# Rotary embedding on one core: first slab loaded in two pieces, the tables behind its first piece on the sync queue, last slab stored in two pieces

## The chip, the cores and the metric

The kernel runs on one core of one Trainium2 chip. The metric is the device time of one execution in microseconds, lower is better; a kernel's time is the median of its runs. Beside the times there is a profile of one execution, taken by the hardware profiler: when each engine's instructions ran, what released them from a wait, and what the DMA engines moved. Times inside a profile count from the start of its span, the first instruction on the core.

## The reference

The input `x` has the shape (8, 2048, 8, 64) in float32: batch, sequence, heads, head dimension. `cos` and `sin` are (2048, 32). Each head's vector of 64 is split into two halves, which are rotated by the position's angles:

```
x1 = x[..., : 32]
x2 = x[..., 32 :]
cos = cos[None, :, None, :]
sin = sin[None, :, None, :]
out1 = x1 * cos - x2 * sin
out2 = x1 * sin + x2 * cos
return concatenate([out1, out2], axis=-1)
```

Input and output are 33.55 MB each, the two tables 0.26 MB each (256 KB). Every element is read once and written once, with three arithmetic operations on it.

## The kernel before

**Tiling.** The sequence of 2048 is cut into 128 partitions of 16 rows each (`R`). One row of a partition is one position: 8 heads of 64, `HD` = 512 floats. Half of a partition's rows (`SL` = 8) of one batch is a slab: 128 partitions by `SLAB` = 4096 floats, 2 MB. There are 16 slabs, numbered 0 to 15 and called x0 to x15 below; their stores are called s0 to s15. Half a slab, `UNIT` = 2048 floats per partition, is 1 MB; `2 * HD` is 512 KB and `HD` is 256 KB.

**Loads.** `load(i)` takes one of `NBUF` = 9 buffers (`xt`) and issues the loads of slab i on the sync queue (SP, line 84), cut as `cuts(i)` says (lines 62 to 65): x0 in 256, 256, 512 and 1024 KB, each other slab in one load of 2 MB. Behind the first piece of x0 the sync queue issues the sin table (line 89). The cos table is issued on the scalar engine's queue (ACT, line 92), ahead of everything else there. Lines 93 and 94 load the first nine slabs at once; slab 9 and those after it are loaded by line 200, when the store of the slab that had the buffer has landed.

**Preparation.** POOL builds an identity matrix (lines 96 and 97). ACT makes `nsin` = -sin (line 106), `neye` (line 107) and `sin_ps`, a copy of sin in PSUM (line 109); DVE copies cos to PSUM as `cos_ps` (line 108).

**Rotation.** `rotate(i, lo, n)` works on one piece of a slab, in place. `pieces(i)` (lines 67 to 72) gives the pieces: x0 in 256, 256, 512 and 1024 KB, x15 in 1024, 512, 256 and 256 KB, every other slab in two of 1 MB. A piece of the usual kind "A" takes four instructions. Two are on POOL (line 138): the halves of `t2`, x times sin and x times -sin with the halves exchanged. Two are on DVE: `t1` = x times cos (line 144) and then `xt` = `t1` + `t2` (line 151). The sum needs both POOL results. `t2` has three buffers, `t1` one in PSUM.

Slabs 5 and 10 are done in another way (`kinds`, lines 114 to 116): their first half is of kind "C" (DVE makes both products, lines 144 and 161), the second of kind "B" (POOL makes `t2` as before), and in both the sum is made on the tensor engine by multiplying with the identity (lines 156, 157, 172, 173), chunk by chunk of 512 floats, and ACT copies each chunk back into `xt` (lines 158 and 176).

**Stores.** `store` issues on the ACT queue (line 183), behind what ACT has been given before it. The loop at line 189 issues the store of slab i - 2 (`LAG` = 2) after the rotation of slab i. So s8 stands on ACT behind the 16 copies of slab 10, and s3 behind the 16 copies of slab 5. In the last round (slab 15) s13 and s14 are issued first, and then each piece of x15 right after its rotation. `keep` holds DVE's and ACT's instructions in program order.

Of the kernel before, what the change touches and what calls it, by code (L numbers as in the profile page):

```python
# [10 lines left out]
def kernel(  # L11
# [7 lines left out]
    nc = tc.nc  # L19
# [7 lines left out]
    HD = H * D  # L27
# [4 lines left out]
    SLAB = SL * HD  # L32
    UNIT = 4 * HD
# [5 lines left out]
    cos_src = cos.rearrange("(q r) d -> q r d", q=P)  # L39
# [10 lines left out]
    cos_sb = const_pool.tile([P, R, Dh], f32, tag="cb")  # L50
# [8 lines left out]
    last = len(slabs) - 1  # L59
    xts = {}  # L60

    def cuts(i):
        if i == 0:
            return [HD, HD, 2 * HD, UNIT]
        return [SLAB]

    def pieces(i):
        if i == 0:
            return [HD, HD, 2 * HD, UNIT]
        if i == last:  # L70
            return [UNIT, 2 * HD, HD, HD]
        return [UNIT, UNIT]

    def spans(sizes):
        lo = 0
        for n in sizes:
            yield lo, n
            lo += n

    def load(i):  # L80
        b, l = slabs[i]
        xt = xpool.tile([P, SLAB], f32, tag="xt", name=f"xt{i}")
        for lo, n in spans(cuts(i)):
            nc.sync.dma_start(
                out=xt[:, lo : lo + n],
                in_=xv[b, :, l * SLAB + lo : l * SLAB + lo + n],
            )
            if i == 0 and lo == 0:
                nc.sync.dma_start(out=sin_sb, in_=sin_src)
        xts[i] = xt  # L90

    nc.scalar.dma_start(out=cos_sb, in_=cos_src)
    for i in range(NBUF):
        load(i)

# [2 lines left out]
        out=eye,  # L98
        in_=eye,
# [80 lines left out]
    def store(i, lo, n):  # L180
        b, l = slabs[i]
        keep(
            nc.scalar.dma_start(  # L183
                out=ov[b, :, l * SLAB + lo : l * SLAB + lo + n],
                in_=xts[i][:, lo : lo + n],
            )
        )

    for i in range(last + 1):
        if i == last:  # L190
            for k in range(i - LAG, i):
                store(k, 0, SLAB)
        for lo, n in spans(pieces(i)):
            rotate(i, lo, n)
            if i == last:
                store(i, lo, n)
        if LAG <= i < last:
            store(i - LAG, 0, SLAB)
        if i > LAG and i - LAG - 1 + NBUF <= last:
            load(i - LAG - 1 + NBUF)  # L200
# [30 lines left out]
```

## Time and profile before

| | |
|---|---|
| median of 4 runs | 164.67 us (164.51 to 164.78) |
| the profiled execution's own time | 164.64 us |
| its span, first to last instruction | 162.9 us |
| DVE busy | 143.4 us, 88% of the span |
| POOL busy | 139.4 us, 86% |
| PE busy | 33.0 us, 20% |
| ACT busy | 12.0 us, 7% |
| moved by DMA | 67.66 MB, mean 415 GB/s over the span |
| loads | 15 of 2 MB, one of 1 MB, one of 512 KB, two of 256 KB; cos and sin 256 KB each |
| stores | 15 of 2 MB, one of 1 MB, one of 512 KB, two of 256 KB |
| DVE, 128x2048: product L144 / sum L151 | 2.293 / 2.292 us |
| DVE, 128x1024: product / sum | 1.229 / 1.225 us |
| DVE, 128x512: product / sum | 0.696 / 0.692 us |
| POOL L138, for a piece of 1 MB / 512 KB / 256 KB | 2.34 / 1.26 / 0.72 us each of two |

Engines are named as in the profile: PE is the tensor engine, DVE the vector engine, ACT the scalar engine, POOL the GpSimd engine, SP the sync engine; a name with q at its end is that engine's sequencer, where DMAs are issued. The row of tenths divides the span into 40 equal slices; a 9 in the row DMA means that the core's 16 DMA engines were busy for 90% of the slice or more. A line of a timeline gives start and duration in us, the engine, the line of the kernel, output and inputs, and in brackets how long the engine had been idle before it and what released it. A DMA's time "to landing" runs from its issue until its completion is signalled.

### The profile page before, as it was taken

The numbers are of one execution on the slowest core, as the hardware profiler recorded it, in microseconds if no ns is written. First come the engines' busy times: TensorE is split into PE (matmuls) and PEld (weight loads), VectorE is DVE, ScalarE is ACT, GpSimd is POOL, SyncE is SP. The second block draws the span as 40 slices with busy tenths as digits, with TensorE's granted clock in tenths as the row PEclk, the third lists the DMA queues.
The fourth block names the chain that finished last, engine by engine and source line by source line (L and its number), as shares of the span: only waits on it lengthen the run. The fifth ranks groups of instructions, "written<-read, shape, count | busy, mean of one in ns | idle before, by whom it ended". The sixth has DMA issues, their size and how long they took to land. (4 is left out here: it accounts for less than half of the span.)

```text
span 162.9 us, 480 instructions
## 1 busy us (share of the span) xinstructions
PE 33.0 (20%) x64; PEld 13.3 (8%) x64; DVE 143.4 (88%) x71; ACT 12.0 (7%) x20; POOL 139.4 (86%) x74
## 2 busy tenths in 40 slices
PE   0000000000000079991000000799940000000000
PEld 0000000000000024440000000234410000000000
DVE  0587999999999999999899999999999999999900
ACT  3300000000000002421000000023220000000000
POOL 1699999999999999799999999956999999995000
PEclk9999999999999999999655555569995555555555
DMA  5999999999999999999999999999999999999995
GB/s 143 390 437 435 427 378 431 435 427 431 439 427 431 431 435 431 427 431 435 427 433 427 433 431 435 427 435 427 435 431 431 427 431 439 427 431 439 419 411 214
DMA packets 5763, 67.66 MB, mean 415 GB/s; under 512 B 640, under 2 KB 640, under 8 KB 1664
## 3 DMA queue, kind: packets, MB, share of 16 engines
q1 hardware_dynamic: 2880, 33.82, 49.6%
q10 hardware_dynamic: 2880, 33.82, 48.8%
q14 instruction: 3, 0.02, 0.0%
HBM read 34.08 MB, written 33.55 MB: 415 GB/s over the span
## 5 line engine op out<-in xcount | busy, mean ns | idle before, releaser
L138 POOL TENSOR_TENSOR t<-xt,sin_sb 128x1024 f32<-128x1024 f32 (+2 forms) x34 | 70.9, 2086 | 10.8 <-DVE xt L151 6.3
L144 DVE TENSOR_TENSOR t<-xt,cos_ps 128x2048 f32<-128x2048 f32 (+2 forms) x36 | 73.9, 2056 | 1.0
L138 POOL TENSOR_TENSOR t<-xt,nsin 128x1024 f32<-128x1024 f32 (+2 forms) x34 | 71.0, 2088 | 0.0
L151 DVE TENSOR_TENSOR xt<-t,t 128x2048 f32<-128x2048 f32 (+2 forms) x32 | 64.8, 2025 | 5.6 <-POOL t L138 2.1
L172 PE MATMUL o<-t,eye 128*128 128x512 f32 x16 | 11.1, 784 | 86.7 <-DVE t L144 86.7
L176 ACT COPY xt<-o 128x512 f32<-128x512 f32 x8 | 4.7, 586 | 95.2 <-PE o L173 95.2
L172 PEld LDWEIGHTS o<-t,eye 128*128 128x128 f32 x16 | 3.7, 244 | 91.4 <-issue 91.4
L156 PE MATMUL o<-t,eye 128*128 128x512 f32 x16 | 8.2, 592 | 0.0
L157 PE MATMUL o<-t,eye 128*128 128x512 f32 x16 | 8.2, 592 | 0.0
L173 PE MATMUL o<-t,neye 128*128 128x512 f32 x8 | 6.2, 862 | 0.2 <-DVE t L161 0.2
L158 ACT COPY xt<-o 128x512 f32<-128x512 f32 x8 | 4.7, 586 | 9.0 <-PE o L157 9.0
L108 DVE COPY cos_ps<-cos_sb 128x512 f32<-128x512 f32 x1 | 0.7, 694 | 4.9 <-DMA cos_sb<-in_cos_dram 4.9
L161 DVE TENSOR_TENSOR t<-xt,sin_ps 128x2048 f32<-128x2048 f32 x2 | 4.6, 2280 | 0.0
L173 PE MATMUL o<-t,eye 128*128 128x512 f32 x8 | 4.1, 592 | 0.0
L157 PEld LDWEIGHTS o<-t,eye 128*128 128x128 f32 x16 | 3.0, 190 | 3.8 <-issue 3.8
L156 PEld LDWEIGHTS o<-t,eye 128*128 128x128 f32 x16 | 3.0, 190 | 3.8 <-issue 3.8
L173 PEld LDWEIGHTS o<-t,neye 128*128 128x128 f32 x8 | 2.1, 287 | 4.8 <-issue 3.2
L173 PEld LDWEIGHTS o<-t,eye 128*128 128x128 f32 x8 | 1.5, 190 | 1.9 <-issue 1.9
L106 ACT ACT_TABLE_LOAD x1 | 1.3, 1283 | 1.2 <-PEq L215 1.2
L106 ACT ACTIVATE nsin<-sin_sb 128x512 f32<-128x512 f32 x1 | 0.6, 630 | 3.1 <-DMA sin_sb<-in_sin_dram 3.1
L109 ACT COPY sin_ps<-sin_sb 128x512 f32<-128x512 f32 x1 | 0.6, 579 | 0.0
L96 POOL MEMSET eye<- 128x128 f32 x1 | 0.2, 205 | 0.3 <-POOLq L215 0.3
(6 smaller groups left out, 1.0 us busy)
## 6 DMA issues: line engine op xcount, KB each, us to landing
xt<-in_x_dram SPq DMA_DIRECT2D x15, 2048.0 KB, 28.3
out_dram<-xt ACTq DMA_DIRECT2D x15, 2048.0 KB, 15.1
xt<-in_x_dram SPq DMA_DIRECT2D x1, 1024.0 KB, 7.6
out_dram<-xt ACTq DMA_DIRECT2D x1, 1024.0 KB, 10.2
xt<-in_x_dram SPq DMA_DIRECT2D x2, 256.0 KB, 4.2
xt<-in_x_dram SPq DMA_DIRECT2D x1, 512.0 KB, 5.6
out_dram<-xt ACTq DMA_DIRECT2D x1, 512.0 KB, 8.9
out_dram<-xt ACTq DMA_DIRECT2D x2, 256.0 KB, 7.5
```

The source lines that it names most:

```text
L106: nc.scalar.mul(nsin, sin_sb, -1.0)
L108: nc.vector.tensor_copy(cos_ps, cos_sb)
L138: nc.gpsimd.tensor_mul(out=t2u[:, :, u, :].rearrange("p (r h) d -> p r h d", h=H), in0=xu[:, :, 1 - u, :].rearrange("p (r h) d -> p r h d" ...
L144: nc.vector.tensor_mul(out=t1.rearrange("p (r k d) -> p r k d", r=nr, d=Dh), in0=xk, in1=rep(cos_ps[:, r0 : r0 + nr, :], 2 * H),)
L151: keep(nc.vector.tensor_add(out=xt, in0=t1, in1=t2))
L156: nc.tensor.matmul(o, eye, t1[:, cs], start=True, stop=False)
L157: nc.tensor.matmul(o, eye, t2[:, cs], start=False, stop=True)
L158: keep(nc.scalar.copy(xt[:, cs], o))
L161: nc.vector.tensor_mul(out=t2.rearrange("p (r k d) -> p r k d", r=nr, d=Dh), in0=xk, in1=rep(sin_ps[:, r0 : r0 + nr, :], 2 * H),)
L172: nc.tensor.matmul(o, eye, t1u[:, gs, u, :], start=True, stop=False)
L173: nc.tensor.matmul(o, eye if u else neye, t2u[:, gs, 1 - u, :], start=False, stop=True)
L176: keep(nc.scalar.copy(xu[:, gs, u, :], o.rearrange("p (g d) -> p g d", d=Dh)))
```

## The change

x0 is loaded in two pieces of 1 MB instead of four, and cos and sin follow its first piece on the sync queue, ahead of the second; nothing is loaded on the scalar queue any more. x0 is rotated in pieces of 512, 512 and 1024 KB (before 256, 256, 512, 1024), and x15 in pieces of 1024, 512 and 512 KB (before 1024, 512, 256, 256). x15 is stored in two pieces of 1 MB, the second after the whole slab's rotation, instead of four pieces each after its own.

```diff
     def cuts(i):
-        if i == 0:
-            return [HD, HD, 2 * HD, UNIT]
-        return [SLAB]
+        return [UNIT, UNIT] if i == 0 else [SLAB]
 
     def pieces(i):
         if i == 0:
-            return [HD, HD, 2 * HD, UNIT]
+            return [2 * HD, 2 * HD, UNIT]
         if i == last:
-            return [UNIT, 2 * HD, HD, HD]
+            return [UNIT, 2 * HD, 2 * HD]
         return [UNIT, UNIT]
...
             if i == 0 and lo == 0:
+                nc.sync.dma_start(out=cos_sb, in_=cos_src)
                 nc.sync.dma_start(out=sin_sb, in_=sin_src)
         xts[i] = xt
 
-    nc.scalar.dma_start(out=cos_sb, in_=cos_src)
     for i in range(NBUF):
         load(i)
...
         for lo, n in spans(pieces(i)):
             rotate(i, lo, n)
-            if i == last:
-                store(i, lo, n)
+            if i == last and lo == 0:
+                store(i, 0, UNIT)
+        if i == last:
+            store(i, UNIT, UNIT)
```

## The prediction

> **What bounds the kernel now.** I read the slices of the page first, then the waits, the start, the chain of waits, and the DMA issues around 120 us. The slices:
>
> ```profile
> PE 33.0 (20%) x64; PEld 13.3 (8%) x64; DVE 143.4 (88%) x71; ACT 12.0 (7%) x20; POOL 139.4 (86%) x74
> DMA  5999999999999999999999999999999999999995
> GB/s 143 390 437 435 427 378 431 435 427 431 439 427 431 431 435 431 427 431 435 427 433 427 433 431 435 427 435 427 435 431 431 427 431 439 427 431 439 419 411 214
> ```
>
> The DMA engines are full from the second slice to the last but one, at some 431 GB/s. 67.66 MB at 431 GB/s are 157 us of the span's 162.9. The rest is the ramp at the start, the end (419, 411, 214) and small dips. So bytes set the time, as long as a transfer is always waiting. DVE is nearly as full: its list of waits has 4.9 us for cos, 2.1 us for POOL, and 0.7 us else. A shift of DVE's start is therefore carried through the kernel; it costs time only where it leaves the DMA engines empty.
>
> The start, in the timeline:
>
> ```profile
> 4.87 0.69 DVE L108 COPY cos_ps<-cos_sb 128x512 f32<-128x512 f32 x1 [4.87 <-DMA cos_sb<-in_cos_dram]
> ...
> 5.67 0.72 POOL L138 TENSOR_TENSOR t<-xt,sin_sb 128x256 f32<-128x256 f32 x1 [4.36 <-DMA sin_sb<-in_sin_dram]
> ...
> 8.39 1.26 POOL L138 TENSOR_TENSOR t<-xt,sin_sb 128x512 f32<-128x512 f32 x1
> ...
> 9.61 1.26 POOL L138 TENSOR_TENSOR t<-xt,nsin 128x512 f32<-128x512 f32 x1
> ...
> 10.82 2.33 POOL L138 TENSOR_TENSOR t<-xt,sin_sb 128x1024 f32<-128x1024 f32 x1
> ...
> 13.09 2.33 POOL L138 TENSOR_TENSOR t<-xt,nsin 128x1024 f32<-128x1024 f32 x1
> ...
> 15.46 2.29 DVE L151 TENSOR_TENSOR xt<-t,t 128x2048 f32<-128x2048 f32 x1 [1.00 <-POOL t L138]
> ```
>
> The reader is to see that POOL, released by sin's landing (5.55), works without a gap, and that DVE's sum at 15.46 is the last for which DVE waits for POOL. From there DVE sets the pace.
>
> The chain of waits names the place where DVE's time meets the DMA engines:
>
> ```profile
> 104.62 0.01 DVE t L144
> ...
> 104.67 2.08 PE o L173 x2
> ...
> 119.09 0.87 PE o L157 x2
> ...
> 119.99 0.02 ACT xt L158
> ...
> 120.05 0.34 ACTq L183
> ...
> 122.89 14.55 DMA out_dram<-xt
> ```
>
> ACT copies slab 10 out behind PE, and s8 stands behind these copies: it is issued at 120.05, though DVE had finished slab 8 long before. No store data moves from about 119 to 121.6 (packet records of the trace); only the last load, x15, does, and the next two rows give its issue at 109.74 and s8's at 120.05:
>
> ```profile
> xt<-in_x_dram SPq DMA_DIRECT2D x1, 2048.0 KB, 13.3
> out_dram<-xt ACTq DMA_DIRECT2D x1, 2048.0 KB, 7.9
> ```
>
> x15 lands at 109.74 + 13.3 = 123.0, s8 at 120.05 + 7.9 = 127.95. So before, s8 is issued while the last load still flows; there is cover, but little: the packet records show each DMA engine taking its first packet of s8 right when its last of x15 ends, the first engine at 121.60 and the last at 122.66. After that only stores are left: 8 slabs, 16.78 MB, 39 us, which is the rest of the span.
>
> **The change part by part.** *The start.* POOL's release is sin's landing. Before it came 5.55, with 0.12 to the first instruction. Now 1 MB of x, cos and sin (1.57 MB in all) come first. Its bounds: before, the third piece of x0 landed 5.6 us after its issue at 2.10, at 7.7, and with it just these 1.57 MB (256 x, cos, sin, 256 x, 512 x); that is the high end. The low end is 1.57 MB at 431 GB/s, 3.65 us, from 2.5 (the first half microsecond above 300 GB/s) plus 0.47 from the last packet to the signal (sin's own: 5.08 and 5.55): 6.6. I take 7.55, near the row of the same bytes, as the slow ramp up to 4 us stays and only packets grow (2 KB ones take 84 ns, 8 KB ones 309, so 0.13 us less in all).
>
> The Trainium skill (DMA: Bandwidth & Descriptors, Anatomy of one DMA) fits, for the GpSimd path, a DMA's time as 2.0 us + bytes / 436 GB/s; that would land 1.57 MB issued from 0.74 at 6.35. The row 7.7 is slower, since the rate needs until about 4 us to reach 390. By the page DVE would be shifted by 0.5 only, and the result would be the first rival's below.
>
> From its release POOL now has four instructions of 512 KB pieces at a spacing of 1.22 (8.39, 9.61, 10.82) and two of 1 MB (2.28 spacing and 2.33): 4 x 1.22 + 4.61 = 9.48. Before it was 4 x 0.68 + 2.43 + 4.61 = 9.76. So POOL is done at 7.55 + 0.12 + 9.48 = 17.15, and DVE's sum that was at 15.46 comes at 17.18: a shift of **1.7 us** (0.8 with the low end, 1.85 with the high). DVE's own work does not set it: cos (earlier in the queue) 0.69, product 1.23, and then it waits for POOL as before. DVE has fewer instructions (6 instead of 8 products and sums on x0), hidden in that wait.
>
> *The queues.* Moving cos off ACT takes 0.41 us of issue from ACT, where nsin waits for sin anyway (3.1 us idle): nothing. On SP it adds 0.43 ahead of sin, but x0's first 1 MB takes 2.4 us to flow, and two issues of 0.43 fall away ahead of x1: nothing; without that cover it would be 0.43. cos itself is now behind 1 MB, and its copy and first product are hidden by POOL's wait for sin.
>
> *DMA bytes.* They stay the same; packets get larger. Head 0.13 and tail (512 + 256 + 256 KB against 1 MB: 8 x 0.159 + 16 x 0.084 - 8 x 0.309 = 0.14) gain 0.27; a dip at 5 to 6 us (348 and 315 GB/s, where the packet size changes) may go, 0.15 more. So if the DMA engines never run dry: -0.4 us, from 0 to -0.6.
>
> *The middle.* With everything DVE does 1.7 later, slab 10 reaches PE at 106.4 instead of 104.67, and the 15.3 us of PE and ACT put s8's issue at 121.75. The last load ends 0.25 earlier, mostly by 121.7. What is late now is s8's first packet. Its lag from issue: at least 0.99 (first load, issue 0.74, first packet 1.73), at most 1.55 (s8 itself, 121.60, held by x15), and the 16 engines started over 0.47 us; for the last engine I take 0.99 + 0.47 = 1.45. So the last engine starts at 123.2 instead of 122.66: +0.54. The DMA engines stand idle some 1 to 1.5 us there, and whatever the head gained is lost in that. From there the 39 us of stores run as before, less the tail's 0.14. **Sum: +0.54 - 0.14 = +0.4 us.** Bounds: with the shift 0.8 no gap (then -0.4); with 1.85 and a lag of 1.55 + 0.47 it is 0.15 + 0.57 more: +1.1.
>
> s3 has the same build, behind slab 5: issued at 73.80, now 75.5, and with 1.45 of lag first data at 77; the loads x0 to x11 last until some 78. Covered by 1 us; if it were not, the loss would be before 121.75 and be swallowed by the gap there.
>
> *The end.* x15's last pieces: DVE needs 2 x 1.23 + gaps = 2.57 for 512 KB instead of 2 x 1.51 for two of 256 KB: 0.46 less. DVE ended at 154.90, now 154.90 + 1.7 - 0.46 = 156.15. The last store, 1 MB, is issued then, against 154.94 for the last 256 KB:
>
> ```profile
> 154.21 0.69 DVE L151 TENSOR_TENSOR xt<-t,t 128x512 f32<-128x512 f32 x1
> ...
> out_dram<-xt ACTq DMA_DIRECT2D x2, 256.0 KB, 7.5
> ```
>
> A quarter of a megabyte took 7 us, so it stood behind other stores. By the packet records some 2.1 MB were left at 156.15 before (more now, as the gap holds them back), 1.1 of them in front of this store: 2.5 us of cover against 1.45 of lag. Nothing; without the cover, 2.43 + 1.45 behind 156.15.
>
> The sum stands against the profiled execution, 164.64 (span 162.9 and 1.8 around it): 165.04. The median is 164.67; I say **165.05**.
>
> **The rivals.** *The gap stays covered, and it gets faster.* One mechanism: the landing of sin. If the ramp is quicker with 8 KB packets and sin lands by 6.8, DVE's shift is below 1.0, s8 is issued by 121.0 with its data by 122.4, under the old 122.66, and the bytes set the end: -0.4, 164.25. For it: at 10 us the rate is 432, and the dip at 5 to 6 belongs to the small pieces. Against: the same bytes took until 7.7. It decides below a shift of some 1.0.
>
> *The two cancel.* Landing near 7.2, shift 1.3: s8's last engine starts at 122.8, +0.15 - 0.14: 164.65.
>
> *The resumed stores take longer.* s3 at 73.80 took 10.4 us to land and s0 14.5, against 4.9 for their bytes. I read this as loads ahead of them in the engines, as the DMA engines stayed full. If 3.4 us of lag (s3's first packet at 77.2) were a price of resuming, s8's data would come at 125.2: +2.5, 167.1. Against it: s8's 1.55.
>
> *The change does not do what it says* (order of the loads): unlikely, as one queue keeps its order.
>
> **How the numbers follow.** Forecast 0.57, of it 0.10 within 0.2% (0.33 us, about what a measurement can tell from no change here); its own range 164.8 to 165.75 (the bound of +1.1). Covered 0.15, of it 0.12 faster by over 0.2% and 0.03 within; cancelling 0.20, all within; long lag 0.08. Faster 0.12, same 0.33, slower 0.55. The range reaches from the covered case to the forecast's upper bound, 164.2 to 165.75, and leaves out the long lag and about half of the covered case.
>
> **What would show it.** sin landing at 7.4 to 7.7; DVE's sum on x0's last piece at 17 to 17.3; L173's start near 106.4 and s8's issue near 121.75; in the windows at 121 to 123 a DMA share clearly below 1 (0.96 or more now); the last store landing 5 to 7 us after its issue, with the slices ahead of it full. If sin lands below 6.9, or no dip shows near 122 while the time is longer, my step is wrong. If DVE waits elsewhere than at x0, or the last store is alone, so is the rest.

## The result, and the profile after

The changed kernel takes 165.20 us (median of 41 runs) where the kernel before takes 164.79 (63 runs): a ratio of 1.0026, 95% interval 1.0017 to 1.0035. It is a quarter of a percent slower, as forecast (165.05). Four of its runs (167.1 to 169.3 us) fell into a slower state that can befall any kernel, and are left out of the ratio and of what follows. The other runs spread from 164.59 to 166.45, wider than before (164.42 to 165.42). The place that the forecast named, however, is not where the time goes.

The page of the changed kernel: its span, the busy share of the DMA engines and their rate in 40 slices.

```profile
span 163.4 us, 460 instructions
...
DMA  5999999999999999999999999999999999999993
GB/s 184 413 449 433 437 305 425 433 429 441 425 429 433 425 441 421 441 425 429 437 421 429 419 423 433 441 421 429 441 421 425 437 441 425 425 441 429 425 413 160
```

The first two slices are better than before (184 and 413, they were 143 and 390), the sixth is worse (305, it was 378), and the last is emptier (160, it was 214) while the span is 0.5 us longer.

The start, in the timeline:

```profile
6.96 2.48 POOL L136 TENSOR_TENSOR t<-xt,sin_sb 128x512 f32<-128x512 f32 x2 [5.65 <-DMA sin_sb<-in_sin_dram]
...
9.39 2.47 POOL L136 TENSOR_TENSOR t<-xt,nsin 128x512 f32<-128x512 f32 x2
...
10.68 1.23 DVE L149 TENSOR_TENSOR xt<-t,t 128x1024 f32<-128x1024 f32 x1 [2.58 <-POOL t L136]
...
16.93 2.29 DVE L149 TENSOR_TENSOR xt<-t,t 128x2048 f32<-128x2048 f32 x1
```

The lines show sin's landing at 6.84, 5.2 us after its issue at 1.62. POOL then made the sin products of the first two pieces together ("x2") and the -sin products after them, so the first piece was complete only behind the third instruction; DVE waited 2.58 us for it. From there DVE went through its own chain without another wait, and the sum of x0's last piece came at 16.93 where it was at 15.46 before: 1.47 us later.

The place where I had forecast a gap, in windows of 1 us of the changed kernel (the last two columns are the DMA share and GB/s):

```profile
121.00:122.00 1.00, 0.00 (x0) 0.00 (x0) 0.97 (x2) 0.00 (x0) 1.00 (x2) 1.00 1.12 475
122.00:123.00 1.00, 0.00 (x0) 0.00 (x0) 1.00 (x1) 0.00 (x0) 1.00 (x1) 1.00 0.84 360
123.00:124.00 1.00, 0.00 (x0) 0.00 (x0) 1.00 (x1) 0.00 (x0) 1.00 (x1) 1.00 1.11 475
```

The mean of the three is 437 GB/s (a single window is uneven, as whole packets of 16 KB fall into one or the next): there is no gap. s8 was issued early enough, as the timeline shows:

```profile
119.62 0.59 ACT L156 COPY xt<-o 128x512 f32<-128x512 f32 x1 [1.13 <-PE o L155]
119.68 4.30 ACTq L181 DMA_DIRECT2D out_dram<-xt  x4
```

It had been at 120.05 before. PE began slab 10 only 1.06 us later than before (105.73 against 104.67 for its second product), and its granted clock rose sooner. In windows at slab 10, the column before the last two is that clock, first in the kernel before, then in the changed one:

```profile
107.00:108.00 1.00, 1.00 (x2) 0.34 (x1) 1.00 (x1) 0.37 (x1) 1.00 (x1) 0.50 1.08 459
108.00:109.00 1.00, 1.00 (x2) 0.34 (x1) 1.00 (x1) 0.00 (x0) 0.18 (x1) 0.50 1.00 426
109.00:110.00 1.00, 1.00 (x4) 0.46 (x3) 0.91 (x2) 0.31 (x1) 0.00 (x0) 1.00 0.99 426
```

```profile
106.00:107.00 1.00, 1.00 (x2) 0.48 (x3) 1.00 (x1) 0.00 (x0) 1.00 (x1) 0.50 0.99 410
107.00:108.00 1.00, 1.00 (x3) 0.44 (x3) 1.00 (x2) 0.40 (x1) 1.00 (x2) 0.90 1.12 475
```

PE's first matmul of slab 10 is at 102.57 before and at 103.63 after. The clock is full at 109.0 before, 6.4 us behind it, and at 107.2 after, 3.6 us behind it. So the stretch at half clock was 2.8 us shorter in the changed kernel's profile.

To see where the time does go, I count what the DMA engines lose in a stretch against their steady 431 GB/s: (431 - rate) / 431 times the stretch, by windows. It is in us of the DMA engines' time, as a mean over the 16.

| stretch, us | 1 to 15 | 15 to 30 | 84 to 95 | 95 to 115 |
|---|---|---|---|---|
| kernel before | 1.98 | 0.63 | 0.00 | 0.00 |
| changed kernel | 1.23 | 1.25 | 0.10 | 0.09 |

The start gains 0.75 us, nearly twice the 0.4 I had given it. Nearly all of it (0.62) is lost by 30 us, where s0, the first store, joins the loads, and 0.2 more by 115 us. In the mean the 16 DMA engines end at the same time as before: at 161.00 us, before at 161.06 (packet records of the trace).

The profiled execution is 0.56 us longer all the same, and that has two parts. The first is the spread of the engines: the first of the 16 ends at 160.41 (before 160.74), the last at 161.99 (before 161.69), 0.30 us later. The last store lands when the slowest engine has ended, at 162.34 (before 162.02). The second part, 0.24 us, lies behind this landing. At the end of the program the sync engine waits for the completion of the stores in five instructions, one after another. Here is its list of waits at this place, first in the kernel before, then in the changed one (us in total, times, longest):

```profile
SPq L226 <- DMA out_dram<-xt: 51.8, 5, 47.0
```

```profile
SPq L226 <- DMA out_dram<-xt: 52.9, 1, 52.9
```

Before, the sync engine waits five times, and the last store is the last that it waits for: it is done with the five 0.08 us after the landing. In the changed kernel the last store signals what the first of the five asks for; the other four have nothing to wait for, but they still run behind it, 0.06 us apart, and the sync engine is done 0.32 us after the landing. It is 0.08 in each profile of the kernel before and its variants, 0.32 or 0.21 in each of the changed kernel and its variants.

### The profile page after: what moved, and what is told of

The parts are those of the page before. It is cut to its first block, busy times and chain, and to the rows that moved or that the text cites. A ratio compares the mean times of both kernels' runs of the same rounds, so it can differ in the third digit from the quotient of the medians.

```text
span 163.4 us, 460 instructions
## 1 busy us (share of the span) xinstructions
PE 31.7 (19%) x64; PEld 12.9 (8%) x64; DVE 142.8 (87%) x67; ACT 12.0 (7%) x20; POOL 138.7 (85%) x70
## 5 line engine op out<-in xcount | busy, mean ns | idle before, releaser
L136 POOL TENSOR_TENSOR t<-xt,sin_sb 128x1024 f32<-128x1024 f32 (+1 forms) x32 | 70.5, 2206 | 10.2 <-DMA sin_sb<-in_sin_dram 5.7
L142 DVE TENSOR_TENSOR t<-xt,cos_ps 128x2048 f32<-128x2048 f32 (+1 forms) x34 | 73.5, 2168 | 1.0
L136 POOL TENSOR_TENSOR t<-xt,nsin 128x1024 f32<-128x1024 f32 (+1 forms) x32 | 70.6, 2209 | 0.0
L149 DVE TENSOR_TENSOR xt<-t,t 128x2048 f32<-128x2048 f32 (+1 forms) x30 | 64.5, 2150 | 5.6 <-POOL t L136 2.6
L170 PE MATMUL o<-t,eye 128*128 128x512 f32 x16 | 10.2, 726 | 87.7 <-DVE t L142 87.7
L155 PE MATMUL o<-t,eye 128*128 128x512 f32 x16 | 8.2, 592 | 0.0
L154 PE MATMUL o<-t,eye 128*128 128x512 f32 x16 | 8.2, 592 | 0.0
L171 PE MATMUL o<-t,neye 128*128 128x512 f32 x8 | 5.7, 800 | 0.1
L171 PE MATMUL o<-t,eye 128*128 128x512 f32 x8 | 4.1, 592 | 0.0
```

Of the source, the lines that this page charges most:

```text
L136: nc.gpsimd.tensor_mul(out=t2u[:, :, u, :].rearrange("p (r h) d -> p r h d", h=H), in0=xu[:, :, 1 - u, :].rearrange("p (r h) d -> p r h d" ...
L142: nc.vector.tensor_mul(out=t1.rearrange("p (r k d) -> p r k d", r=nr, d=Dh), in0=xk, in1=rep(cos_ps[:, r0 : r0 + nr, :], 2 * H),)
L149: keep(nc.vector.tensor_add(out=xt, in0=t1, in1=t2))
L154: nc.tensor.matmul(o, eye, t1[:, cs], start=True, stop=False)
L155: nc.tensor.matmul(o, eye, t2[:, cs], start=False, stop=True)
L170: nc.tensor.matmul(o, eye, t1u[:, gs, u, :], start=True, stop=False)
```

## The experiments

Twelve kernels, in three sets; each set shares its runs of the kernel before. "Loss" is counted as above.

**The changed kernel again (r1).** No edit.

> The changed kernel unaltered, for a second profile and its spread. Theory A (cover at 122 us): in executions in which PE's granted clock rises late in slab 10's chain (mean granted clock near 0.782) s8 is issued near 121.1 and the time is about 0.5 us longer than in those in which it rises early (mean clock near 0.799, s8 at 119.7). Theory B (first store): every execution has the slow stretch of the loads between 21 and 24.5 us (305 GB/s in that slice, 378 in the kernel before) and so the same extra 0.3 to 0.6 us, whatever the clock. Ratio near 1.0026.

Ratio 1.0042 (1.0020 to 1.0065). The losses: 1.01 us from 15 to 30 and 0.48 from 84 to 95, where it had been 0.10. All runs list the mean granted clock of PE, and its values gather in two groups, near 0.782 and 0.799. (The mean counts the time before PE's first work as full clock.) The groups are only a rough mark of a late clock at slab 5: the clock is full 3.5 us after PE's first matmul there in the changed kernel's profile and 4.9 after it in r1's (means 0.797 and 0.801), but 5.4 in r2's and 5.8 in r4's (0.781 and 0.783). In the other 38 runs listed with the result, the 25 with a mean clock over 0.79 have a median of 164.96, the 13 below it one of 165.58; here it is 164.97 (6) against 166.08 (6). The kernel before hardly cares: 164.85 (14) and 164.84 (15) in this set, 164.78 (18) and 164.99 (17), 164.69 (12) and 164.79 (17) in the two others. So the half of theory A that concerns the clock holds as far as this: a low mean clock goes with a longer time. Whether s8 is the place is asked by r4.

**cos back on the scalar queue (r2), and the old end (r3).**

```diff
             if i == 0 and lo == 0:
-                nc.sync.dma_start(out=cos_sb, in_=cos_src)
                 nc.sync.dma_start(out=sin_sb, in_=sin_src)
...
+    nc.scalar.dma_start(out=cos_sb, in_=cos_src)
     for i in range(NBUF):
```

> Only the cos load goes back to the scalar queue; x0 in two pieces and the new tail stay. Theory A: sin lands 0.3 to 0.6 us earlier, less delay of DVE, so 0.1 to 0.4 us faster than the changed kernel. Theory B, if the slow stretch at 21 to 24.5 us comes from the scalar queue carrying nothing before its first store: the slice goes back to about 378 GB/s, the last store's engines end together again and the time falls by 0.3 to 0.6 us, to a ratio of 1.000. If the slow stretch comes from the first store and a load being issued at the same moment (19.25 and 19.11), or from something else, the slice stays near 305 and the ratio near 1.002.

Ratio 1.0035 (1.0020 to 1.0051), not to be told from r1's 1.0042. sin landed at 6.96, not earlier than in the changed kernel (6.84). The loss from 15 to 30 us is 0.94: a scalar queue that has carried a load does not cure it. Moving one load between the queues changes nothing that can be measured here. The Trainium skill (DMA: Bandwidth & Descriptors, Issuing engines are not separate DMA queues) says that such a move only saves the time of issuing; the ratios of r1 and r2 agree.

```diff
         if i == last:
-            return [UNIT, 2 * HD, 2 * HD]
+            return [UNIT, 2 * HD, HD, HD]
...
-            if i == last and lo == 0:
-                store(i, 0, UNIT)
-        if i == last:
-            store(i, UNIT, UNIT)
+            if i == last:
+                store(i, lo, n)
```

> Only the end goes back: x15 rotated in 1024, 512, 256, 256 KB and stored in four pieces. My sum gave the new tail a gain of 0.14 us (fewer, larger packets) behind a cover of 2.5 us, so this kernel is 0.1 to 0.2 us slower than the changed one, ratio near 1.0035. A rival, that the single 1 MB store at the end costs time, expects it faster, ratio 1.001 or less.

Ratio 1.0049 (1.0030 to 1.0068), against r1's 1.0042: on the expected side, but inside the intervals. The new end is worth nothing that these runs can show. The cover of 2.5 us fits this, but the waits behind the last landing take 0.21 us in r3 and 0.32 in r1, so by that measure the new end costs 0.11 us.

**s8 ahead of slab 10's copies (r4).**

```diff
+        if i in (10,):
+            store(i - LAG, 0, SLAB)
         for lo, n in spans(pieces(i)):
             rotate(i, lo, n)
...
-        if LAG <= i < last:
+        if LAG <= i < last and i not in (10,):
             store(i - LAG, 0, SLAB)
```

> Changed kernel, but s8 is issued on ACT ahead of slab 10's copies instead of behind them, so that stores wait while the last load flows. Theory A: the late-clock executions lose their extra 0.5 us, the spread shrinks, the median falls by 0.2 to 0.4 us to a ratio of 1.000 to 1.001. Theory B: nothing changes, ratio 1.0026, since the loss happened at 21 to 24 us.

Ratio 1.0045 (1.0027 to 1.0063): no gain. With s8 issued at 91.95 there is no gap at 122, and yet the runs with a low mean clock still take 165.65 (9 runs) against 164.84 (3). Theory A's place, s8, falls. Its profile, and that of r2, show another: a slow stretch near 88 us. The windows of r2:

```profile
87.00:88.00 1.00, 0.00 (x0) 0.00 (x0) 0.97 (x2) 0.00 (x0) 1.00 (x1) 0.50 1.02 262
88.00:89.00 1.00, 0.00 (x0) 0.00 (x0) 1.00 (x1) 0.00 (x0) 1.00 (x1) 0.50 0.86 311
89.00:90.00 1.00, 0.00 (x0) 0.00 (x0) 0.90 (x2) 0.00 (x0) 1.00 (x2) 0.50 0.89 377
```

There the load of x12 joins the stores s3 to s7. It had to wait for the landing of s3, and s3 stands behind slab 5's copies on ACT, as s8 does behind slab 10's (eight copies a slab by the timeline, not 16). Sorted by the issue of s3, the loss from 84 to 95 us in the profiles up to here is: 73.80, 0.00 (before); 75.31, 0.10 (changed); 75.56, 0.15 (r3); 76.15, 0.48 (r1); 76.38, 0.79 (r2); 76.54, 0.77 (r4). Three later profiles in which s3 stands behind copies add 75.12, 0.03 (r8); 75.60, 0.41 (r7); 76.25, 0.15 (r9). So by and large the loss grows with the lateness of s3, with r9 as the exception. The issue of s3 depends on PE's clock. Here are the last copy of slab 5 and s3's issue, in the changed kernel and then in r4:

```profile
75.30 0.59 ACT L156 COPY xt<-o 128x512 f32<-128x512 f32 x1 [1.13 <-PE o L155]
75.31 7.45 ACTq L181 DMA_DIRECT2D out_dram<-xt  x5
```

```profile
76.53 0.59 ACT L156 COPY xt<-o 128x512 f32<-128x512 f32 x1 [1.13 <-PE o L155]
76.54 6.47 ACTq L181 DMA_DIRECT2D out_dram<-xt  x5
```

PE began slab 5 at nearly the same time in both (59.36 and 59.45), but its clock was full from 62.8 in the one and from 65.2 in the other (by the clock records of the traces; the pace of ACT agrees, whose first two copies start at 63.28 and 65.00 in the one and at 63.66 and 66.23 in the other). So DVE's delay of 1.5 us and a late clock of 1.2 us add up to 2.7 for s3.

**s3 and s8 ahead of the copies, in the changed kernel (r5, r12) and in the kernel before (r6).** The edit is that of r4 with (5, 10) in place of (10,).

> Changed kernel with s3 issued ahead of slab 5's copies and s8 ahead of slab 10's. Theory C: what varies is a slow stretch of the DMA engines near 88 us, where x12's load joins stores that were resumed late (s3 issued at 75.3 to 76.5 us, loss 0.15 to 0.8 us of DMA time between 84 and 95 us in four profiles, the more the later s3). With s3 not behind the copies no store is resumed late: the loss between 84 and 95 us falls below 0.1, executions with a late PE clock are no slower than those with an early one, and the ratio falls to 1.000 to 1.002. Theory A (s8 alone) was at 1.0045 with s8 first and expects that again.

> The kernel of r5 again beside r10 and r11 on one chip: ratio 0.9985 to 1.0005, loss between 84 and 95 us below 0.1, whatever the PE clock.

> The same move in the kernel before. Theory C: its loss between 84 and 95 us is 0.05 already, so no change, ratio 0.999 to 1.001. If the resumed stores cost the kernel before anything, it gets faster than 0.999.

Ratios 0.9994 (0.9985 to 1.0004), 1.0003 (0.9993 to 1.0013) and 1.0001 (0.9988 to 1.0015). s3 is now issued as soon as slab 3 is done:

```profile
47.66 0.34 ACTq L181 DMA_DIRECT2D out_dram<-xt  x1
```

The stretch from 84 to 95 us, first in r4, then in r5 (the last column is GB/s):

```profile
84.00:95.00 11.00, 0.00 (x0) 0.00 (x0) 10.62 (x6) 0.00 (x0) 11.00 (x6) 0.50 1.00 401
```

```profile
84.00:95.00 11.00, 0.00 (x0) 0.00 (x0) 10.63 (x6) 0.00 (x0) 11.00 (x6) 0.50 1.00 428
```

The loss there is 0.08 in r5 and 0.03 in r12, and the clock no longer matters: 164.78 (6 runs) and 164.75 (5) in r5. r4 and r5 differ by the place of s3 alone, 1.0045 against 0.9994. So s3 behind the copies costs the changed kernel 0.4 to 0.8 us (1.0026 and 1.0045 against 1.0003 and 0.9994). The kernel before, where s3 comes 1.5 us earlier, gains nothing from the same move.

How a late s3 does it is not shown. Its first data leave at 77.23 us in the kernel before, 1.3 us before the first engine ends x11's load; in the changed kernel they leave at 77.67 and in r4 at 77.63, just as x11 ends, whatever the issue. No gap opens there (431 GB/s from 75 to 84 us before, 428 in the changed kernel, 433 in r4), and x12's load is issued at 84.29, 83.71 and 83.55, so no later than before. What does change is the issuing of the stores behind s3: from 73.80 on ACT issues four in 1.89 us in the kernel before, from 76.15 on two in 2.65 us in r1. r5 also takes away more than the lateness: x12's load is issued at 64.26 there and follows x11 without a pause, so that there is no joining of a running store queue.

With s3 first, the last DMA engine ends at 161.51 (r5) and 161.43 (r12), 0.2 to 0.3 us before that of the kernel before (161.69). The 0.24 us of waits behind the last landing use that up, and the time is the same.

**s3 made late in the kernel before (r9).** `scr` is a small tile in SBUF.

```diff
             if i == last:
                 store(i, lo, n)
-        if LAG <= i < last:
+            if i == 7 and lo == 0:
+                keep(nc.scalar.copy(scr, xts[7][:, 0:8]))
+                store(3, 0, SLAB)
+                store(4, 0, SLAB)
+                load(12)
+        if LAG <= i < last and i not in (5, 6):
             store(i - LAG, 0, SLAB)
-        if i > LAG and i - LAG - 1 + NBUF <= last:
+        if i > LAG and i != 6 and i - LAG - 1 + NBUF <= last:
```

> Kernel before, with s3 (and s4 and x12's load behind it) held back on ACT until the first half of slab 7 is rotated, so that s3 is issued at 76.2 to 76.6 us instead of 73.8; nothing else is later. Theory C says that this lateness alone makes the slow stretch where x12's load joins: loss between 84 and 95 us 0.6 to 0.8 us instead of 0.05, time longer by 0.4 to 0.9 us, ratio 1.003 to 1.005. Rival: the loss belongs to the changed start or to the deeper DVE delay, and this kernel stays at 1.000.

```profile
76.24 0.20 ACT L199 COPY scr<-xt 128x8 f32<-128x8 f32 x1 [0.73 <-DVE xt L152]
76.25 6.71 ACTq L184 DMA_DIRECT2D out_dram<-xt  x5
```

Ratio 1.0103 (1.0083 to 1.0123): 1.8 us longer, twice what I had expected at most. That holding back s3, and with it s4 and the order for x12, costs time is shown; DVE's end is where it was. But the loss sits elsewhere than expected: only 0.15 us from 84 to 95. The end shows it, first r9's windows, then those of the kernel before:

```profile
161.00:162.00 1.00, 0.00 (x0) 0.00 (x0) 0.00 (x0) 0.00 (x0) 0.00 (x0) 0.50 0.29 111
162.00:163.00 1.00, 0.00 (x0) 0.00 (x0) 0.00 (x0) 0.00 (x0) 0.00 (x0) 0.50 0.12 49
163.00:164.00 1.00, 0.00 (x0) 0.00 (x0) 0.00 (x0) 0.00 (x0) 0.00 (x0) 0.50 0.10 37
```

```profile
161.00:162.00 1.00, 0.00 (x0) 0.00 (x0) 0.00 (x0) 0.00 (x0) 0.00 (x0) 0.50 0.11 41
162.00:163.00 1.00, 0.00 (x0) 0.00 (x0) 0.00 (x0) 0.00 (x0) 0.00 (x0) 0.50 0.00 0
```

A DMA share of 0.12 is two of 16 engines. By the packet records the engines' ends lie between 161.18 and 163.83. Their mean is 0.9 us later than before (161.98 against 161.06), the last 2.1, so a loss counted as a mean over the 16 understates it. The engines part late: the load of x14 still ends within 1 us on all of them (117.15 to 118.10), that of x15 at 122.0 to 122.3 on 14 engines and at 125.3 and 126.0 on two. That is where s8 joins, not where x12 does. So r9 shows that a late s3 can cost time, but not that it does so in the way of the changed kernel: in r1, r2 and r4 the mean of the ends is late (161.31 to 161.57, in r5 160.76), and their spread is small (1.1 to 1.3 us).

**The first store (r7, r8, r10, r11).** Why does the changed kernel lose 1.0 to 1.25 us around s0 where the kernel before loses 0.6? r7 holds s0 back in the changed kernel until the first half of slab 1 is rotated, r8 in the kernel before until its first product is done.

```diff
+        if i == LAG:
+            keep(nc.scalar.copy(scr, xts[1][:, 0:8]))
         if LAG <= i < last:
```

> Changed kernel in which s0 is held back on ACT until the first half of slab 1 is rotated (a copy of 8 columns), so from 19.3 to 24.0 us, while x7's load is still issued at 19.1 to 19.2. Theory D (the first store and a load issued within 0.2 us of each other hamper each other): the loss at the first store falls from 1.1 to 0.6 us or less, ratio 1.001. Rival E (the loss belongs to the first store beside five queued loads of 2 MB, whenever it comes): the slow stretch moves by 4.7 us and keeps its 1.0 to 1.2 us, ratio 1.003 or more.

```diff
+        if i == 1 and lo == 0:
+            keep(nc.scalar.copy(scr, t1[:, 0:8]))
         if kind == "A":
```

> Kernel before in which s0 is held back until the first product of slab 1 is done (20.1 us instead of 17.8), so that it is issued within 0.2 us of x7's load (19.98). Theory D: the loss at the first store grows from 0.60 to about 1.1 us and the time by 0.3 to 0.5 us, ratio 1.002 to 1.003. Rival E: loss stays near 0.6, or follows the number of loads queued, ratio 1.000 to 1.001.

r7: ratio 1.0042 (1.0024 to 1.0059), loss 1.11, and the slow stretch moves with s0. From 21 to 24 us the rate is now 426 GB/s (273 in the changed kernel), from 27 to 30 it is 311 (431). By itself r7 doesn't decide, as x8's load was issued at 24.11, again within 0.1 us of s0. r8 speaks against the coincidence, theory D: s0 at 20.29 and x7 at 20.06, 0.23 us apart (in the changed kernel 19.25 and 19.11), loss 0.49 where theory D expected 1.1, ratio 0.9998 (0.9987 to 1.0009).

r10 and r11 start from r5's kernel. r10 loads x0 in the four pieces of before; r11 issues x6, x7 and x8 on the scalar queue behind s0, s1 and s2.

```diff
     def cuts(i):
-        return [UNIT, UNIT] if i == 0 else [SLAB]
+        return [HD, HD, 2 * HD, UNIT] if i == 0 else [SLAB]
```

> Changed kernel with s3 and s8 first, and x0 loaded in the four pieces of before (cos and sin still behind the first one on the sync queue). Asks which part of the start gives the gain of 0.66 us in the first 15 us and which the extra 0.55 us of loss at the first store. If both belong to the cut of x0: head loss 1.8, loss at the first store 0.6, ratio 0.999 to 1.000. If the gain belongs to the order in one queue: head loss near 1.2.

Ratio 1.0030 (1.0017 to 1.0043), against r12's 1.0003 on the same chip. The loss is 1.95 us from 1 to 15 (r12: 1.3) and 0.97 from 15 to 30 (1.11). So the gain of the start belongs to the cut of x0 into two, and it is worth some 0.4 us (165.18 against 164.78). The extra loss at the first store, however, does not belong to it, and so the ratio that I expected with it, 0.999 to 1.000, is missed.

```diff
-    for i in range(NBUF):
+    for i in range(6):
         load(i)
...
             store(i - LAG, 0, SLAB)
+        if i in (2, 3, 4):
+            load(i + 4, nc.scalar)
```

> Changed kernel with s3 and s8 first, and the loads of x6, x7, x8 issued on the scalar queue behind s0, s1 and s2 instead of ahead on the sync queue. If the loss at the first store comes from the loads queued beside it (about 4.9 of 2 MB), it falls with 2.9 queued from 1.1 us to 0.6 or less, and the ratio from 0.9994 to 0.995 to 0.997. Rival: the loss is that of any first store beside a full load queue; it stays at 1.0 to 1.2 and the ratio at 0.999 to 1.000.

Ratio 0.9996 (0.9982 to 1.0010), loss 1.04: the loads queued beside s0 are not the cause. What makes the first store dearer in the changed kernel stays open; r8 all but takes the near issue of a load off the list, r2 an unused scalar queue, r10 the cut of x0, r11 the number of queued loads. No version beats the kernel before by more than its interval.

## Why the prediction was right, and where it was not

*What bounds the kernel*: right. The DMA engines set the time, and a shift of DVE costs where it disturbs them.

*The release of POOL*: my bounds for sin's landing were 6.6 to 7.7; I took 7.55 and it was 6.84, under the 6.9 that I had called a failure of the step. The row I leaned on, the same bytes in small pieces, was too slow a guide: larger pieces also gained in the ramp (229 and 410 GB/s from 2 to 3 and 3 to 4 us, before 174 and 356). The estimate by the fit of the Trainium skill (DMA: Bandwidth & Descriptors, Anatomy of one DMA), 6.35, was 0.5 below the measurement, my value 0.7 above it.

*DVE's shift of 1.7*: 1.47, close, with two errors that cancel. sin came 0.7 earlier, and POOL's new order, in which both pieces' sin products come first, made DVE's own chain the longer one. I had taken the order from the source; the program's order on POOL was another. With sin at 6.84 and the order that I had assumed, my own sum gives a shift of 1.0. By slab 10 the shift was 1.06, as the kernel before has an idle 0.52 us on DVE at 79 that the changed one doesn't have there.

*The middle* is the step that failed: "the DMA engines stand idle some 1 to 1.5 us there". s8 was issued at 119.68 (120.52 in r1), not at 121.75, and neither profile of the changed kernel has a gap at 122. I had carried PE's 15.3 us over as a constant; it was 13.9. r4 shows that s8 is not the place at all, since putting it first changes nothing. In its place stands the step that I had written off, s3: "covered by 1 us; if it were not, the loss would be before 121.75 and be swallowed". The same cause, a store behind ACT's copies made late by DVE's shift, works there (r4 against r5). It does not empty the DMA engines: the cover of s3 was just enough, and the loss comes some 10 us later, when x12 joins, in a way that stays open. The gap at 122 that was to swallow it never came.

*The gain of the head*: I had 0.27 in packets and 0.15 in a dip; windows show 0.75. *The first store* was not in the sum: 0.6 more lost, for a reason that stays open. These two nearly cancel, which is luck.

*The end*: right as to the store, which landed 6.8 us after its issue at 155.54, behind others. But "nothing" was not the price of the end: the sync engine's waits behind this landing took 0.24 us more than before, over half of the 0.41 us by which the medians differ. No term of the sum has them.

*The rivals*: "the gap stays covered" came true as to the gap, but not its 164.25, as s3 and the first store took the gain. "The two cancel" counted on a later sin and a gap of s8, and neither came. The long lag of resumed stores was not seen: s3's first data left 3.4 us after its issue in the kernel before, 2.4 in the changed one and 1.1 in r4; a fixed price of resuming would not shrink.

So 165.05 against 165.20 rests on a right direction of cause (later DVE, later stores behind ACT) and a wrong place; that the number came so close is luck. +0.54 at 122 us and -0.14 at the tail were added up. In the profile it was about 0.75 gained at the head, 0.62 lost at the first store and 0.2 from 84 to 115 us, which leaves the mean engine where it was; then 0.30 for the slowest engine and 0.24 for the waits behind it.

## What to carry to other kernels

In a kernel that fills the DMA engines, what a change does to the order and time at which one queue joins the other can be worth as much as it gains elsewhere (0.6 us at the first store against 0.75 at the head); look at each place where a queue starts beside a running one, at the slowest of the 16 engines at the end, not only at the mean rate, and at what still runs behind the last landing. A store that stands on an engine's queue behind copies inherits every delay of those copies' producers, PE's clock among them; issuing it ahead of them (r5) took away both the loss and the spread. And read an engine's order from the built program, not from the source.

## What the runs showed of the hardware

PE's granted clock rises at different distances from the first matmul in executions of one program: at slab 5 by 3.5 us in the changed kernel's profile and by 4.9 in r1's. Over all profiles it is 3.3 (slab 5 of the kernel before) to 6.4 us (its slab 10). The Trainium skill (TensorE: Matmul & The Clock Gate, Part 1: The HAM clock gate) explains it with a free-running window of 3.4 us and gives a spread of 0.5 us to either side; the window agrees (the stretches of full clock in the profiles last 17.07 or 13.65 us, 5 or 4 times 3.413), the spread here is larger. In the changed kernel a low mean clock goes with 0.6 us more of the whole time, through s3: with s3 ahead of the copies (r5) the difference is gone.

The store queue that starts beside the full load queue costs 0.5 to 1.25 us of the DMA engines' time around it in these profiles, and this moves with the store (r7).

The sync engine's waits for the stores at the end of the program run one after another, some 0.06 us each, also when there is nothing left to wait for. Where the last store signals the first of them, 0.32 us pass from its landing (changed kernel), where it signals the last, 0.08 (kernel before), and 0.21 where two stand behind it (r3, r10).
